# The second half's attention: its scores in pairs of PSUM banks, with one maximum and one exponential for each tile

## The chip, the cores and the metric

The kernel runs on one core of one Trainium2 chip. Its time is the device time of one execution in microseconds (us). The engines are TensorE (PE, with its weight loads as PEld), VectorE (DVE), ScalarE (ACT), GpSimd (POOL) and SyncE (SP), which issues most of the DMAs. Each engine works through a queue of its own in order, and semaphores tie the queues together. TensorE writes into PSUM, which has eight banks of 128 partitions x 512 floats.

## The reference, cut to what matters

One inference step of a decoder layer: 1024 prompt rows of width 1024, and beside them one new row for each of 8 samples, which attend over 8192 past positions in a paged cache. Both groups go through a combined projection, forgetting attention (8 heads of 64) and spatial gating, a merge, cross-attention to 256 memory rows, and a gated MLP of 2816 columns. The change is in the attention of the prompt:

```python
def fox_attend(q, k, v, cq, ck, qpos, kpos):
    s = jnp.einsum('bqhd,bkhd->bhqk', q, k).astype(jnp.float32) * (ATT_HEAD_DIM ** -0.5)
    s = s + (cq.astype(jnp.float32).transpose(0, 2, 1)[:, :, :, None]
             - ck.astype(jnp.float32).transpose(0, 2, 1)[:, :, None, :])
    s = jnp.where(kpos[None, :] <= qpos[:, None], s, -jnp.inf)
    p = jax.nn.softmax(s, axis=-1).astype(v.dtype)
    return jnp.einsum('bhqk,bkhd->bqhd', p, v)
```

cq and ck are running sums of the logarithm of the forget gate. Inputs and outputs are float32.

## The kernel before

**Stages.** The prompt is worked on in two halves of 512 rows. `prompt` (L1701) goes through the projections (p1), the attention of the first half (att0) and of the second (att1), and then for each half the merge with cross-attention (mid0, mid1) and the MLP (ffn0, ffn1). The 8 samples are a background: the main loop lets one step of theirs in whenever the prompt's work has passed a pace that is set for each stage (`PACE`). A step of the samples gathers pages of the cache by GpSimd (L1306 for keys, L1365 for values), multiplies keys and query on VectorE (L1312), sums these products there (L1316), or multiplies values with weights on TensorE (L1371). In att1 the key products and sums are cut into pieces of 1024 elements (`KS` = 2).

**The order of the instructions.** The program is built in a tile framework: the code gives out tiles of named pools, the framework puts a wait wherever a buffer is used again, and a planner that knows costs of its own for the instructions fixes the order of each engine's queue when the kernel is built. The code's order is its start; instructions of different stages and of the background can change places.

**PSUM before.** One pool holds all eight banks: four single banks under the tag `ba` (`BA()`, L115), two under `bb`, one under `ms`, one under `dv`. `BK()` (L123) hands out `ba` and `bb` in turn to the large matmuls of the other stages. A buffer of a tag is given out again once all reads of its last tile are done.

**The attention of a half** (`attention(hf)`, L657; hf = 1 is the second half, rows 512 to 1023). Heads are taken in pairs, hp = 0 to 3, and rows in two blocks (blk) of two query blocks of 128 rows each (ii), for each of the two heads of a pair (j). That makes eight score tiles for each head pair: 640, 768, 640 and 768 keys wide, and then 896, 1024, 896 and 1024; 32 tiles in the half. In the first half of the prompt tiles are 128 to 512 keys wide and fit one bank.

- `setup` (L674) prepares a head pair while the one before it runs: four transposes of q (L677) into a `ba` bank, copies to SBUF on ScalarE (L683, L684), and a subtraction on VectorE (L697) that gives the low parts; then twice, for the two halves of the keys, four transposes (L702) into a `ba` bank, copies on ScalarE (L706), casts on GpSimd (L708) and subtractions on VectorE (L713). Two matmuls with high and low parts then give float32 precision.
- `scores` (L716) makes a tile. Its width is cut into two halves of n = 320, 384, 448 or 512 columns, each in a `ba` bank of its own: matmuls L728 and L730, the causal mask by a matmul L732 on the second half, and a maximum of each half on VectorE (L733). L736 joins the two maxima (they are negated, so by a minimum). Then ScalarE takes the exponential of each half (L738), which adds up its row as it goes; the sums come out with an accumulator read, and lie in `ls`. The result goes to a slot shared with streamed weights (`wr`, four slots).
- `turn` (L749) transposes the exponentials (L756) into `bb` and `ms` banks and copies them out, on ScalarE (L763) or for one in four on VectorE (L761).
- `values` (L765) multiplies with v (L772), copies the result (L781), adds up the halves' sums (L783) and takes the reciprocal (L784); `back` (L787) transposes (L793) and scales (L795).

`turn`, `values` and `back` stand in a list that runs two tiles behind the scores (`LA`), so that between a tile's scores and its transposes the next two tiles' scores are issued:

```python
queue.append(partial(turn, p_, pt[j], nkt - 1 + ii, ii))
...
drain(LA[hf])
yield 1.8
```

Beside att1 runs the end of the first half (`close`, L863, by `beside`, L879), and after it follow the merge (L860) and its output projection (L973 to L975).

Of the kernel before, what the change touches and what calls it, by code (L numbers as in the profile page):

```python
# [7 lines left out]
F32 = mybir.dt.float32  # L8
# [3 lines left out]
AF = mybir.ActivationFunctionType  # L12
ALU = mybir.AluOpType
AX = mybir.AxisListType
PSUM = bass.MemoryType.PSUM
# [3 lines left out]
P = 128  # L19
# [59 lines left out]
def build(nc, tc, ctx, a, phases=None):  # L79
# [8 lines left out]
    psum = ctx.enter_context(tc.tile_pool(name="psum", bufs=1, space=PSUM))  # L88
    dram = ctx.enter_context(tc.tile_pool(name="dram", bufs=1, space=DRAM))

    cnt = [0]

    def nm(s):
        cnt[0] += 1
        return f"{s}_{cnt[0]}"
# [16 lines left out]
    def sm(shape, tag, bufs=2, dt=F32):  # L112
        return small.tile(shape, dt, tag=tag, bufs=bufs, name=nm(tag))

    def BA():  # L115
        return psum.tile([P, 512], F32, tag="ba", bufs=4, name=nm("ba"))

    def BB():
        return psum.tile([P, 512], F32, tag="bb", bufs=2 + MB, name=nm("bb"))
# [537 lines left out]
    def attention(hf, late=None, at=3):  # L657
# [58 lines left out]
        def scores(qkv, ls, blk, j, ii):  # L716

            qab, ka, kb, _ = qkv
            i = blk * 2 + ii
            e = (hf * 4 + i + 1) * P  # L720
            nch = 1 if e <= 512 else 2
            n = e // nch
            p_ = (WRAW(e) if PW else U([P, e])) if hf else T2(e)
            mx = sm([P, 2], "mx", 4)
            tiles = []
            for ch in range(nch):
                s = BA()[:, :n]
                mmul(s, qab[j][:, 0, i * P : (i + 1) * P], ka[j][:, ch * n : ch * n + n], start=True, stop=False)  # L728
                diag = ch == nch - 1
                mmul(s, qab[j][0:68, 1, i * P : (i + 1) * P], kb[j][0:68, ch * n : ch * n + n], start=False, stop=not diag)  # L730
                if diag:
                    mmul(s[:, n - P :], ident_b, cmask_b, start=False, stop=True)  # L732
                nc.vector.tensor_reduce(mx[:, ch : ch + 1], s, axis=AX.X, op=ALU.max, negate=True)  # L733
                tiles.append(s)
            if nch == 2:
                nc.vector.tensor_tensor(mx[:, 0:1], mx[:, 0:1], mx[:, 1:2], op=ALU.min)  # L736
            for ch in range(nch):
                nc.scalar.activation(  # L738
                    p_[:, ch * n : ch * n + n], tiles[ch], AF.Exp, bias=mx[:, 0:1], accum_out=ls[:, ii, j, ch : ch + 1]
                )  # L740
            return p_

# [22 lines left out]
        def values(qkv, ls, pt, hp, blk):  # L765
            vn = qkv[3]
            nkt = hf * 4 + blk * 2 + 2
            po = B3()
            for kt in range(nkt):
                for j in range(2):  # L770
                    q0 = P if kt == nkt - 1 else 0
                    mmul(  # L772
                        po[64 * j : 64 * j + 64, q0:256],
                        vn[:, kt, 64 * j : 64 * j + 64],
                        pt[j][kt // 4][:, kt % 4, q0:256],
                        start=(kt == 0),
                        stop=(kt == nkt - 1),
                        tile_position=(0, 64 * j),
                    )
            ot = T2(256)  # L780
            nc.scalar.activation(ot, po[:, :256], AF.Copy)  # L781
            rl = sm([P, 4], "rl", 3)
            nc.vector.tensor_reduce(rl, ls.rearrange("p i j c -> p (i j) c"), axis=AX.X, op=ALU.add)  # L783
            nc.vector.reciprocal(rl, rl)  # L784
            return ot, rl, hp, blk

        def back(ot, rl, hp, blk):  # L787
# [25 lines left out]
        for hp in range(4):  # L813
            for _ in nxt or ():
                pass
            qkv, nxt = got.pop(), None
            if hp == at and late:
                late()
            for blk in range(2):
                ls = sm([P, 2, 2, 2], "ls", 3)  # L820
                if hf == 0:
                    nc.vector.memset(ls, 0.0)
                pt = []
                nkt = hf * 4 + blk * 2 + 2
                for j in range(2):
                    for ii in range(2):
                        p_ = scores(qkv, ls, blk, j, ii)
                        if ii == 0:
                            pt.append(
                                [  # L830
                                    (U([P, 4, 256]) if nkt - g > 2 else T2(512).rearrange("p (a b) -> p a b", b=256))
                                    for g in range(0, nkt, 4)
                                ]
                            )
                        queue.append(partial(turn, p_, pt[j], nkt - 1 + ii, ii))
                        if j == 1 and ii == 1:

                            def fin(*args):
                                r = values(*args)
                                queue.insert(min(BKQ, len(queue)), partial(back, *r))  # L840

                            queue.append(partial(fin, qkv, ls, pt, hp, blk))
                        drain(LA[hf])
                        yield 1.8
                        if hp < 3 and (blk, j, ii) == LD[hf]:
                            raw = load(hp + 1)
                        if hp < 3 and (blk, j, ii) == ST[hf]:
                            nxt = setup(hp + 1, *raw)
                        if nxt:
                            next(nxt, None)  # L850
                            yield 1
# [11 lines left out]
    def close(hf, att):  # L863

        ssa = sm([P, 4], "ssa", 1)
        for i in range(4):
            ssq_into(ssa[:, i : i + 1], att[i // 2][:, i % 2, :])
        yield
        r = rstd_of(ssa, AW, 4, "ra")
        yield  # L870
        for b2 in range(2):
            for i in range(2):
                t = att[b2][:, i, :]
                nc.vector.tensor_scalar(t, t, r[:, b2 * 2 + i : b2 * 2 + i + 1], None, op0=ALU.mult)
            t0 = hf * 4 + b2 * 2
            nc.sync.dma_start(an_d[t0 * P : (t0 + 2) * P, :].rearrange("(c p) d -> p c d", p=P), att[b2])
        yield

    def beside(main, steps, at):  # L879

        n = 0
        while True:
            try:
                t = next(main)
            except StopIteration as e:
                return e.value
            yield t
            if n in at:
                next(steps)
            n += 1  # L890
# [810 lines left out]
    def prompt():  # L1701
# [26 lines left out]
        ending = close(0, att)  # L1728
        next(ending)
        phase[0] = "att1"  # L1730
        if G0R:
            att = yield from mix(gating(0), att1, 1 / G0R)
        else:
            att = yield from beside(att1, ending, (0, 2))
        ending = close(1, att)
        next(ending)
        ends = []
# [133 lines left out]
```

## Time and profile before

| | |
|---|---|
| median of 3 runs | 1911.37 us (1909.26 to 1916.39) |
| the profiled execution | 1913.18 us, span 1911.4 us |
| mean granted TensorE clock | 0.978 of full speed |
| PE busy | 1816.1 us, 95% of the span |
| PEld busy | 1296.3 us, 68% |
| DVE busy | 1404.6 us, 73% |
| ACT busy | 761.7 us, 40% |
| POOL busy | 480.6 us, 25% |
| moved by DMA | 517.07 MB, 271 GB/s in the mean |

Busy time leaves out register, branch, semaphore and DMA-issuing instructions. In the rows of the profile, `L728 ... ba<-u,u 128*128 128x448 f32` is line 728 with output and input by the names in the code (`ba` is a bank of that tag, `u` a work tile, `wr` a slot for weights and exponentials, `mx` the maxima, `ls` the sums), then the shape of what is written or read. What stands in brackets at the end of a row of the timeline is the time for which the engine was idle just before, and what ended it. In a group, "10.8, 689 | 6.5" is busy time in us, the mean of one instruction in ns, and the engine's idle time ahead of the group. A group's releaser is inferred from semaphores.

### The profile page before, as it was taken

The page shows a single profiled execution, that of the slowest core. Times are in us where ns is not written, and L with a number is a line of the kernel's source. Part 1 is how long each engine was busy: PE and PEld are TensorE (multiplying, and loading weights), DVE is VectorE, ACT ScalarE, POOL GpSimd, SP SyncE. Part 2 cuts the span into 40 slices and gives each one's busy share as a digit, 9 for nine tenths or more (in the row PEclk, how much of TensorE's full clock was granted, in tenths as well). Part 3 has the DMA queues.
Part 4 walks back from the last instruction along what each step waited for, and adds up shares of the span by engine and source line. Part 5 has one row for each costly group of instructions (what it writes and reads, how often), then busy time and mean ns, then how long its engine had stood idle before and what let it go on. Part 6 is the DMA issues. An engine that isn't in the chain of part 4 may idle for free.

```text
span 1911.4 us, 24216 instructions
## 1 busy us (share of the span) xinstructions
PE 1816.1 (95%) x9255; PEld 1296.3 (68%) x9255; DVE 1404.6 (73%) x1662; ACT 761.7 (40%) x1435; POOL 480.6 (25%) x429
## 2 busy tenths in 40 slices
PE   8999999778898999999999999998999999899998
PEld 5987666555676667777777776775665667667765
DVE  4888678777777887989989998887864548754344
ACT  5332356566633435333333244324353333232232
POOL 1232342222121332213432322354222012101110
PEclk9999999989998999999999999998999999899999
DMA  8777988743395876759878879888859557676872
GB/s 322 286 245 278 323 319 302 265 162 119 128 399 210 324 268 256 297 206 359 313 264 313 301 304 344 340 338 302 307 206 362 191 200 265 215 242 247 320 280 101
DMA packets 156373, 517.07 MB, mean 271 GB/s; under 512 B 20169, under 2 KB 41929, under 8 KB 123489
## 3 DMA queue, kind: packets, MB, share of 16 engines
q0 software_dynamic: 56400, 339.04, 47.7%
q1 hardware_dynamic: 92944, 163.89, 24.7%
q10 hardware_dynamic: 6912, 12.59, 1.7%
q8 instruction: 73, 1.20, 0.2%
q14 instruction: 44, 0.35, 0.1%
HBM read 493.63 MB, written 21.84 MB: 270 GB/s over the span
## 4 chain that ended last, share of the span: by engine, by line
PE 66%; DVE 8%; ACT 3%; DMA 3%; issue 2%; POOL 0%; SPq 0%; DVEq 0%; POOLq 0%; ACTq 0%
PE ba L247 9%; PE ba L246 9%; PE ba L248 9%; PE bb L246 6%; PE bb L247 5%; PE bb L248 5%; PE dv L1371 5%; DMA kv<-cache_k,kidx 2%; DVE kv L1312 1%; DVE s L1316 1%; PE dv L1614 1%; PE ba L973 1%; PE ba L975 1%; PE ba L974 1%; PE bb L772 1%
## 5 line engine op out<-in xcount | busy, mean ns | idle before, releaser
L209 ACT ACTIVATE wh<-wr 128x1024 fp32r<-128x1024 f32 (+2 forms) x220 | 228.8, 1044 | 488.8 <-PE ba L247 147.8
L210 DVE TENSOR_TENSOR wl<-wr,wh 128x1024 fp32r<-128x1024 f32 (+2 forms) x220 | 262.5, 1200 | 166.7 <-PE ba L248 71.3
L1306 POOL DMA_INDIRECT kv<-cache_k,kidx x128 | 179.8, 1405 | 545.6 <-DVE s L1316 249.3
L1312 DVE TENSOR_TENSOR kv<-kv,d 128x2048 f32<-128x2048 f32 (+1 forms) x139 | 292.3, 2113 | 28.2 <-DMA kv<-cache_k,kidx 26.9
L1316 DVE TENSOR_REDUCE s<-kv 128x32 f32<-128x2048 f32 (+1 forms) x139 | 292.0, 2106 | 0.6
L1365 POOL DMA_INDIRECT kv<-cache_v,kidx x128 | 181.3, 1416 | 424.2 <-PE dv L1371 169.6
L246 PE MATMUL ba<-wh,u 128*128 128x512 f32 (+1 forms) x596 | 226.9, 382 | 0.0
L247 PE MATMUL ba<-wl,u 128*128 128x512 f32 (+1 forms) x596 | 226.2, 380 | 0.0
L248 PE MATMUL ba<-wh,u 128*128 128x512 f32 (+1 forms) x596 | 223.4, 380 | 1.0 <-DVE u L210 1.0
L246 PE MATMUL ba<-u,wh 128*128 128x512 f32 (+2 forms) x520 | 203.0, 391 | 1.3 <-DVE u L213 1.2
L247 PE MATMUL ba<-u,wh 128*128 128x512 f32 (+2 forms) x520 | 203.8, 392 | 0.0
L248 PE MATMUL ba<-u,wl 128*128 128x512 f32 (+2 forms) x520 | 202.7, 390 | 0.0
L1371 PE MATMUL dv<-kv,s 128*32 128x512 f32 x1024 | 138.0, 618 | 6.8 <-DMA kv<-cache_v,kidx 6.8
L246 PE MATMUL bb<-u,wh 128*128 128x512 f32 (+2 forms) x344 | 138.2, 402 | 1.8 <-DVE u L213 1.8
L247 PE MATMUL bb<-u,wh 128*128 128x512 f32 (+2 forms) x344 | 136.5, 397 | 2.5 <-DVE u L213 2.5
L248 PE MATMUL bb<-u,wl 128*128 128x512 f32 (+2 forms) x344 | 135.9, 396 | 0.0
L246 PEld LDWEIGHTS ba<-wh,u 128*128 128x128 f32 x596 | 112.7, 189 | 31.4 <-issue 8.0
L248 PEld LDWEIGHTS ba<-wh,u 128*128 128x128 f32 x596 | 112.1, 189 | 29.0 <-issue 6.3
L247 PEld LDWEIGHTS ba<-wl,u 128*128 128x128 f32 x596 | 112.4, 189 | 23.8 <-issue 2.9
L247 PEld LDWEIGHTS ba<-u,wh 128*128 128x128 f32 x520 | 98.7, 190 | 33.3 <-issue 13.0
L246 PEld LDWEIGHTS ba<-u,wh 128*128 128x128 f32 x520 | 98.5, 190 | 31.7 <-issue 7.1
L248 PEld LDWEIGHTS ba<-u,wl 128*128 128x128 f32 x520 | 98.5, 189 | 28.5 <-issue 9.3
(418 smaller groups left out, 3105.5 us busy)
## 6 DMA issues: line engine op xcount, KB each, us to landing
wr<-w_up SPq DMA_DIRECT2D x88, 512.0 KB
kv<-w_up POOLq DMA_DIRECT2D x22, 1024.0 KB
wr<-w_down SPq DMA_DIRECT2D x40, 512.0 KB
kv<-w_down POOLq DMA_DIRECT2D x11, 1024.0 KB
wr<-w_in SPq DMA_DIRECT2D x16, 512.0 KB
wr<-w_o SPq DMA_DIRECT2D x16, 512.0 KB
wr<-w_cq SPq DMA_DIRECT2D x16, 512.0 KB
wr<-w_co SPq DMA_DIRECT2D x16, 512.0 KB
```

What stands on the lines that cost most here:

```text
L209: nc.scalar.activation(h, src, AF.Copy)
L210: nc.vector.tensor_tensor(l, src, h.bitcast(F32), op=ALU.subtract)
L246: mmul(out, sh, mh, start=(i == 0), stop=False)
L247: mmul(out, sh, ml, start=False, stop=False)
L248: mmul(out, sl, mh, start=False, stop=(i == n - 1))
L772: mmul(po[64 * j : 64 * j + 64, q0:256], vn[:, kt, 64 * j : 64 * j + 64], pt[j][kt // 4][:, kt % 4, q0:256], start=(kt == 0), stop=(kt == ...
L973: mmul(pss[i], mh[k][:, tb], wh, start=(k == korder[0]), stop=False)
L1306: nc.gpsimd.indirect_dma_start(kv, None, a["cache_k"], off(kidx[:, b, ch : ch + 1]))
L1312: nc.vector.tensor_tensor(kvv[:, i : i + m, :], kvv[:, i : i + m, :], qb.unsqueeze(1).broadcast_to((P, m, 512)), op=ALU.mult)
L1316: nc.vector.tensor_reduce(s[:, ch * 4 + i : ch * 4 + i + m, :].rearrange("p k h -> p (k h)"), kvv[:, i : i + m, :].rearrange("p k (h d) -> ...
L1365: nc.gpsimd.indirect_dma_start(kv, None, a["cache_v"], off(kidx[:, b, ch : ch + 1]))
L1371: mmul(dv[32 * j : 32 * j + 32, :], s[:, ch * 4 : ch * 4 + 4, :].rearrange("p k h -> p (k h)"), kvv[:, j, :], start=(ch == 0), stop=(ch == ...
```

## The change

The four `ba` banks move into a pool of their own, which is opened and closed by `ba_pool`. For all stages but att1 it holds four single banks, as before. Ahead of att1 it is closed and opened again with two tiles of two banks each, and after att1 it goes back to four. With pairs, `BA()` gives the first half of a pair and, if nothing else came between, the second half the next time; `BA2()` gives a whole pair and drops a half left over. The pair is reused as one tile, when all reads of it are done.

In `scores` a tile of the second half takes a pair, each half of its columns in one bank of it. One maximum on VectorE reads both banks, and one exponential on ScalarE reads both and adds up the whole row. The minimum that joined two maxima is gone, and with it the sum over the halves in `values` and the zeroing of `ls` in the first half; the reciprocal reads `ls` itself. The matmuls are the same. The transposes of `setup` take their bank from `BA()` as before, which in att1 is a half of a pair.

```diff
--- before.py
+++ after.py
@@ -88,6 +88,20 @@
     psum = ctx.enter_context(tc.tile_pool(name="psum", bufs=1, space=PSUM))
     dram = ctx.enter_context(tc.tile_pool(name="dram", bufs=1, space=DRAM))
 
+
+    banks, half_ = [], []
+
+    def ba_pool(pairs):
+        half_.clear()
+        if banks:
+            banks.pop()[0].__exit__(None, None, None)
+        if pairs is not None:
+            p = tc.tile_pool(name="ba2" if pairs else "ba1", bufs=1, space=PSUM, reuse_waits="tile")
+            banks.append((p, p.__enter__(), pairs))
+
+    ba_pool(False)
+    ctx.callback(ba_pool, None)
+
     cnt = [0]
 
     def nm(s):
@@ -113,7 +127,16 @@
         return small.tile(shape, dt, tag=tag, bufs=bufs, name=nm(tag))
 
     def BA():
-        return psum.tile([P, 512], F32, tag="ba", bufs=4, name=nm("ba"))
+        if not banks[0][2]:
+            return banks[0][1].tile([P, 512], F32, tag="ba", bufs=4, name=nm("ba"))
+        if half_:
+            return half_.pop()[:, 512:]
+        half_.append(BA2())
+        return half_[0][:, :512]
+
+    def BA2():
+        half_.clear()
+        return banks[0][1].tile([P, 1024], F32, tag="ba", bufs=2, name=nm("ba"))
 
     def BB():
         return psum.tile([P, 512], F32, tag="bb", bufs=2 + MB, name=nm("bb"))
@@ -721,22 +744,22 @@
             nch = 1 if e <= 512 else 2
             n = e // nch
             p_ = (WRAW(e) if PW else U([P, e])) if hf else T2(e)
-            mx = sm([P, 2], "mx", 4)
-            tiles = []
+            mx = sm([P, 1], "mx", 4)
+            both = BA2().rearrange("p (c n) -> p c n", c=2)[:, :, :n] if nch == 2 else BA()[:, :n].unsqueeze(1)
             for ch in range(nch):
-                s = BA()[:, :n]
+                s = both[:, ch, :]
                 mmul(s, qab[j][:, 0, i * P : (i + 1) * P], ka[j][:, ch * n : ch * n + n], start=True, stop=False)
                 diag = ch == nch - 1
                 mmul(s, qab[j][0:68, 1, i * P : (i + 1) * P], kb[j][0:68, ch * n : ch * n + n], start=False, stop=not diag)
                 if diag:
                     mmul(s[:, n - P :], ident_b, cmask_b, start=False, stop=True)
-                nc.vector.tensor_reduce(mx[:, ch : ch + 1], s, axis=AX.X, op=ALU.max, negate=True)
-                tiles.append(s)
-            if nch == 2:
-                nc.vector.tensor_tensor(mx[:, 0:1], mx[:, 0:1], mx[:, 1:2], op=ALU.min)
-            for ch in range(nch):
+            if nch == 1:
+                nc.vector.tensor_reduce(mx, s, axis=AX.X, op=ALU.max, negate=True)
+                nc.scalar.activation(p_[:, :e], s, AF.Exp, bias=mx, accum_out=ls[:, ii, j : j + 1])
+            else:
+                nc.vector.tensor_reduce(mx, both, axis=AX.XY, op=ALU.max, negate=True)
                 nc.scalar.activation(
-                    p_[:, ch * n : ch * n + n], tiles[ch], AF.Exp, bias=mx[:, 0:1], accum_out=ls[:, ii, j, ch : ch + 1]
+                    p_[:, :e].rearrange("p (c n) -> p c n", c=2), both, AF.Exp, bias=mx, accum_out=ls[:, ii, j : j + 1]
                 )
             return p_
 
@@ -780,8 +803,7 @@
             ot = T2(256)
             nc.scalar.activation(ot, po[:, :256], AF.Copy)
             rl = sm([P, 4], "rl", 3)
-            nc.vector.tensor_reduce(rl, ls.rearrange("p i j c -> p (i j) c"), axis=AX.X, op=ALU.add)
-            nc.vector.reciprocal(rl, rl)
+            nc.vector.reciprocal(rl, ls.rearrange("p i j -> p (i j)"))
             return ot, rl, hp, blk
 
         def back(ot, rl, hp, blk):
@@ -817,9 +839,7 @@
             if hp == at and late:
                 late()
             for blk in range(2):
-                ls = sm([P, 2, 2, 2], "ls", 3)
-                if hf == 0:
-                    nc.vector.memset(ls, 0.0)
+                ls = sm([P, 2, 2], "ls", 3)
                 pt = []
                 nkt = hf * 4 + blk * 2 + 2
                 for j in range(2):
@@ -1728,10 +1748,12 @@
         ending = close(0, att)
         next(ending)
         phase[0] = "att1"
+        ba_pool(True)
         if G0R:
             att = yield from mix(gating(0), att1, 1 / G0R)
         else:
             att = yield from beside(att1, ending, (0, 2))
+        ba_pool(False)
         ending = close(1, att)
         next(ending)
         ends = []
```

## The prediction

> **What bounds the kernel now.** I read the page first, then busy time by stretches, then TensorE's waits inside the stretch that the diff touches, then the timeline around the longest of them. The stretch is 390 to 527 us: the profile's first pair of 320-wide score matmuls starts just before it and the last tile's products end with it. In the stretches the columns are start:end, length, busy time of PE, PEld, DVE, ACT and POOL (with instructions), granted TensorE clock, DMA share and GB/s.
>
> ```profile
> span 1911.4 us, 24216 instructions
> PE 1816.1 (95%) x9255; PEld 1296.3 (68%) x9255; DVE 1404.6 (73%) x1662; ACT 761.7 (40%) x1435; POOL 480.6 (25%) x429
> 390.00:527.00 137.00, 111.45 (x751) 77.88 (x750) 99.13 (x201) 88.49 (x235) 29.11 (x37) 0.93 0.43 145
> 620.00:760.00 140.00, 134.70 (x650) 95.26 (x648) 112.67 (x119) 65.37 (x137) 41.91 (x34) 0.99 0.78 291
> ```
>
> TensorE is busy for 95% of the span, and 134.70 of 140.00 us in a stretch after the change: what the second half's attention saves or loses, the rest passes on to the end. In that stage TensorE is idle for 137.00 - 111.45 = 25.55 us, and at a clock of 0.93 a further 111.45 x 0.07 = 7.8 us are lost. These 33 us are all that a better order could win. DMA moves 145 GB/s, so transfers are not the matter. VectorE and ScalarE aren't full, but TensorE waits for them:
>
> ```profile
> PE ba L728 <- DVE mx L736: 6.8, 1, 6.8
> PE ba L728 <- ACT wr L738: 5.6, 6, 1.6
> 416.12 1.29 DVE L733 TENSOR_REDUCE mx<-ba 128x1 f32<-128x512 f32 x2
> 417.32 1.21 DVE L1316 TENSOR_REDUCE s<-kv 128x16 f32<-128x1024 f32 x1
> ...
> 419.98 1.20 DVE L1316 TENSOR_REDUCE s<-kv 128x16 f32<-128x1024 f32 x1
> ...
> 421.82 0.14 DVE L736 TENSOR_TENSOR mx<-mx 128x1 f32<-128x1 f32 x1
> 422.00 0.69 ACT L738 ACTIVATE wr<-ba,mx 128x512 f32<-128x512 f32 x1 [6.02 <-DVE mx L736]
> 422.05 0.71 PE L728 MATMUL ba<-u,u 128*128 128x448 f32 x1 [6.78 <-DVE mx L736]
> ```
>
> The first two rows are total, times and longest. The timeline shows the largest: both maxima of a 1024-wide tile are done by 417.4, but the small minimum that joins them (L736) stands on VectorE behind two halves of the decoder's key products, and everything waits to 422.
>
> **What the change costs and saves, part by part.** In the built program the order of every engine is the one before up to the end of the first half's attention, and again from some 60 us behind the second's (TensorE's first 1788 and last 5170 of 8073 instructions are equal). DMA issues are equal in number; within the stage one V gather moves ahead of two casts (L708) on POOL, and single loads change place with a neighbour on SP. At 145 GB/s I cost that at nothing; were a gather late by one cast, it is 0.65 us.
>
> Fewer instructions. Here and below the form 128x512 is a half of a 1024-wide tile:
>
> ```profile
> L733 DVE TENSOR_REDUCE mx<-ba 128x1 f32<-128x512 f32 x16 | 10.8, 689 | 6.5 <-PE ba L730 3.5 <-PE ba L732 2.7
> L733 DVE TENSOR_REDUCE mx<-ba 128x1 f32<-128x128 f32 x8 | 2.3, 284 | 0.1
> L736 DVE TENSOR_TENSOR mx<-mx 128x1 f32<-128x1 f32 x32 | 4.7, 152 | 0.4
> L783 DVE TENSOR_REDUCE rl<-ls 128x4 f32<-128x8 f32 x9 | 1.4, 157 | 3.9 <-ACT wr L738 3.9
> L738 ACT ACTIVATE wr<-ba,mx 128x512 f32<-128x512 f32 x16 | 10.9, 692 | 10.9 <-DVE mx L736 10.9
> L738 ACT ACTIVATE wr<-ba,mx 128x320 f32<-128x320 f32 x16 | 8.3, 534 | 0.0
> L738 ACT ACTIVATION_READ_ACCUMULATOR wr<-ba,mx 128x1 f32 x64 | 13.3, 208 | 0.0
> L1082 DVE TENSOR_REDUCE cmx<-ba 128x2 f32<-128x512 f32 x12 | 8.1, 684 | 5.5 <-PE ba L1080 3.4 <-issue 2.1
> ```
>
> A maximum costs (689 - 284) / 384 = 1.05 ns per element and 149 ns besides; an exponential (692 - 534) / 192 = 0.82 and 271. So one maximum over a pair of 512 is an estimated 149 + 1.05 x 1024 = 1.23 us and one exponential 271 + 0.82 x 1024 = 1.11. Per tile VectorE saves 149 + 152 = 0.30 us, ScalarE 271 + 208 = 0.48. Over 32 tiles that is 9.6 and 15.3 us; eight L783 add 1.3 (the memsets of ls and L783 in the first half save VectorE little, where TensorE waits for others). None of it is on the path by itself. No row reads two banks at once. Bounds: as dear as two single instructions (1.38 and 1.38 us, so +0.42 us per tile on the chain), or as the fit; L1082, with a grouped read, costs no more than the plain one (684 against 689), so I take the fit.
>
> Later banks. From the tile's last matmul, the first half's bank came free after 0.69 + 0.15 + 0.69 = 1.53 us, now with the second after 1.23 + 1.11 = 2.34. So the first is 0.8 us later, the second about as before. There are two pairs. In the built program each group of transposes that sets up the next head pair (L677 once, L702 twice, three times over) takes one of the two pairs for half its width. TensorE works in order, so behind a waiting score matmul stand the transposes, products and decoder matmuls of other tiles, and VectorE and ScalarE soon wait for those. The places, before:
>
> ```profile
> 401.25 0.44 PE L728 MATMUL ba<-u,u 128*128 128x384 f32 x1 [1.35 <-ACT wr L738]
> 405.11 0.47 PE L728 MATMUL ba<-u,u 128*128 128x448 f32 x1 [0.55 <-ACT wr L738]
> 406.67 1.92 PE L1371 MATMUL dv<-kv,s 128*32 128x512 f32 x16
> 443.82 3.42 PE L772 MATMUL ms<-u,u 128*64 128x256 f32 x16 [2.79 <-ACT t L763]
> 449.72 0.60 PE L702 MATMUL ba<-cp,u 128*128 128x128 f32 x4
> 450.16 0.38 PE L793 MATMUL ms<-cp,t 128*128 128x128 f32 x2
> 450.46 1.20 ACT L706 ACTIVATE u<-ba 64x512 fp32r<-64x512 f32 x2
> 451.69 0.69 ACT L738 ACTIVATE wr<-ba,mx 128x512 f32<-128x512 f32 x1
> 451.72 1.38 DVE L713 TENSOR_TENSOR u<-ba,u 64x512 fp32r<-64x512 f32 x2
> 452.52 0.47 PE L728 MATMUL ba<-u,u 128*128 128x448 f32 x1 [1.56 <-ACT wr L738]
> 474.75 0.65 PE L772 MATMUL bb<-u,u 128*64 128x256 f32 x2 [0.52 <-DVE t L761]
> 476.26 1.72 PE L772 MATMUL bb<-u,u 128*64 128x256 f32 x13 [0.86 <-ACT u L763]
> 483.44 0.47 PE L728 MATMUL ba<-u,u 128*128 128x448 f32 x1 [1.56 <-ACT wr L738]
> 487.17 2.35 DVE L1312 TENSOR_TENSOR kv<-kv,d 128x1024 f32<-128x1024 f32 x2
> 490.83 2.33 DVE L1316 TENSOR_REDUCE s<-kv 128x16 f32<-128x1024 f32 x2
> 494.10 0.65 PE L756 MATMUL bb<-cp,wr 128*128 128x128 f32 x4 [3.96 <-ACT wr L738]
> ```
>
> (a) The second 896-wide tile of head pairs 0, 1 and 2 waited 6.78, 1.56 and 1.56 us. It now lies on the pair of the 1024-wide tile right ahead of it, with only four transposes (449.72 to 450.16, 0.44 us) between. Behind these come two L706 (1.20) on ScalarE, then the exponential (1.11) and a hand-over of 0.14 (451.69 + 0.69 to 452.52): 0.44 + 0.10 + 1.20 + 1.11 + 0.14 = 3.0 from the tile's last matmul, so TensorE is idle for 3.0 - 0.44 = 2.55, three times. The minimum behind the key products is gone, but this comes in its place: 7.65 - 9.90 = -2.25 us.
>
> (b) The value products L772 wait for ScalarE's copies (L763), which stand behind the set-up's four copies: 2.79 us at 443.82, 0.52 + 0.86 at 475, and nothing in head pair 0, where eight decoder matmuls (1.92 at 406.67) filled the time. In the new order these eight stand behind the L772, because the transposes ahead of them need the pair. I take the mean of the two shown, 2.1, three times: 6.3 - 4.2 = +2.1.
>
> (c) The last tile of head pair 2 had its minimum behind two L1312 and two L1316 (487.17 to 493.2); its maximum now stands there in one piece: 2.35 + 2.33 + 1.23 + 1.11 + 0.14 = 7.2 against 494.10 - 487.17 = 6.9: +0.3.
>
> (d) The third and fourth tile (401.25, 405.11) waited 1.35 + 0.55; the first bank comes 0.8 later: +0.8. The first tile needs the bank of the first half's last tile, under seven transposes: nothing; without these, 0.7.
>
> (e) The second L702 group lies on the first one's pair and waits for its L713 (1.38 for two), which it didn't before: between 0 and 1.4 three times; 2.0, since VectorE's queue is long there.
>
> (f) The clock. After a long wait TensorE runs slow for a while:
>
> ```profile
> 400.00:405.00 5.00, 3.30 (x22) 2.54 (x22) 3.17 (x11) 5.00 (x18) 3.97 (x6) 1.00 0.58 204
> 420.00:425.00 5.00, 2.95 (x10) 2.28 (x11) 3.41 (x7) 2.30 (x7) 0.96 (x1) 0.50 0.88 249
> 425.00:430.00 5.00, 4.34 (x30) 3.44 (x29) 2.88 (x9) 3.49 (x10) 0.00 (x0) 0.86 0.64 237
> 450.00:455.00 5.00, 3.44 (x20) 2.52 (x19) 4.29 (x11) 4.34 (x12) 1.22 (x2) 0.87 0.36 110
> ```
>
> The wait of 1.35 us at 401 left it at 1.00; that of 1.56 at 452 was followed by 0.87, that of 6.78 by 0.50 and 0.86. Five waits of 1.56 or more cost the 7.8 us, 1.56 each. Now they are (a) three, (b) three, (c) one: two more, +3.1, less about one share for the 6.78 that becomes 2.55: +1.5. [...]
>
> (g) Shorter queues: each copy that (b) waits for stands behind one exponential, now 0.48 shorter, three times 1.4; the small waits of the stage (25.55 - 9.90 - 4.2 - 3.96 - 1.90 = 5.6 us in about ten) lose an estimated 0.15 each: -2.9 together.
>
> Sum: -2.25 + 2.1 + 0.3 + 0.8 + 2.0 + 1.5 - 2.9 = +1.6 us.
>
> The profiled execution took 1913.18 us, 1.8 more than its span; so 1914.8 for it, and from the median of the runs (1911.37, 0.1% below it) **1913.0**.
>
> **The rivals.**
>
> Faster: the pairs do not bind, and what waited for VectorE and ScalarE gains. For it: 25 us less work on two engines that end nearly all of TensorE's waits. Against it: the order gives (a) new waits where the old went. Priced: 6.78 becomes 2.55 (-4.2), 3.96 becomes 2.5 as the key products slip behind (-1.5), three slow-clock shares go (-4.7): -10.4, 1901.0.
>
> Slower: two pairs are too few. Each of the nine set-up groups holds one, so score tiles go one at a time. Three of the nine are in (a); at the six others TensorE waits a whole 2.34 + 0.14 less some seven transposes (0.11 each, 0.8), 1.7 each, 10.2, and two more slow-clock shares (3.1): +13.3 on the forecast's base, 1924.7. It decides once TensorE has under 2.5 us of other work between two tiles on one pair. Against it: the order puts six to ten transposes and the value products there. [...]
>
> Two-bank reads at the dear end: +0.42 on the chain at about ten waits, +4.2: 1917.2.
>
> It changes nothing at the end, because a later wait takes up the difference: 1911.4. TensorE's 134.70 of 140.00 speaks against it.
>
> **How the numbers follow.** Forecast 0.39, faster rival 0.22, slower rival 0.32, dear reads 0.04, nothing 0.03: the rivals together get more than half, since the terms (b), (e) and (g) are each about as large as the sum. The range takes in both rivals' prices: 1900 to 1926. I leave out 0.2, gains or losses beyond them. [...] About 0.5% (9.6 us) is what a measurement of this kernel can tell from no change. Faster by more: the faster rival, 0.22; slower: the slower one, 0.32; within it the rest, 0.46.
>
> **What would show it.** Right: in the changed profile 32 maxima near 1.23, 1.09, 0.96 and 0.82 us and 32 exponentials near 1.11 to 0.80; VectorE's work in the stage 10 to 11 us less, ScalarE's 15 less; no wait of 6.8 us; three waits near 2.5 on the second 896-wide tile, ended by the exponential; L772 waiting in head pair 0; a stage of 137 us within 4, at a clock of 0.91 to 0.94. Wrong: idle time below 18 or above 36 us in the stage, or a difference that arises outside it.

## The result, and the profile after

The changed kernel takes 1903.99 us (median of 14 runs, 1895.07 to 1908.88) against 1910.84 us for the kernel before beside it (14 runs, 1906.80 to 1916.39): a ratio of 0.995, 95% interval 0.9939 to 0.9961 (the two medians alone give 0.9964). By the medians it is some 7 us faster, at the edge of the 0.5% that the prediction took as the least that can be told. The forecast was 1913.0, slower by 1.6 us; the time lies in the range, on the other side. The profiled execution took 1899.86 us, 4 us less than the median, so what follows looks at stretches and not at its span alone.

The first line of the page, and the stretches, which are cut here for each kernel by its own landmarks: from the first 320-wide score matmul to the end of the last products (the attention), and from the first matmul of the first output projection to that of the second (behind the attention). First the kernel before, with columns as in the prediction:

```profile
389.20:525.90 136.70, 111.15 (x749) 77.46 (x747) 99.28 (x201) 88.38 (x235) 29.11 (x37) 0.93 0.42 142
526.70:690.00 163.30, 153.07 (x733) 108.47 (x731) 127.24 (x137) 68.98 (x141) 39.55 (x31) 0.97 0.81 302
```

The changed kernel:

```profile
span 1898.1 us, 24082 instructions
```

and its stretches:

```profile
388.90:520.50 131.60, 111.92 (x732) 79.41 (x731) 88.74 (x126) 79.55 (x164) 31.93 (x37) 0.90 0.43 146
521.20:679.60 158.40, 152.51 (x732) 108.91 (x731) 127.19 (x137) 69.12 (x140) 45.96 (x31) 0.98 0.84 311
```

The attention lasts 131.6 us and not 136.7: TensorE's idle time in it fell from 25.55 to 19.68 us, while the mean granted clock fell from 0.93 to 0.90. The stretch behind lasts 158.4 and not 163.3, though VectorE does the same work there (127.19 against 127.24 us in 137 instructions). So in this profile nearly as much was gained in a stretch where the code wasn't touched as in the attention.

The new instructions, by line and shape, are as large as the prediction's fit made them (1.23 and 1.11 us for 1024 elements, 0.82 for the maximum of 640):

```profile
L760 DVE TENSOR_REDUCE mx<-ba 128x1 f32<-128x1024 f32 x8 | 9.8, 1224 | 3.8 <-PE ba L755 3.7
L760 DVE TENSOR_REDUCE mx<-ba 128x1 f32<-128x640 f32 x8 | 6.5, 814 | 6.0 <-PE ba L755 6.0
L761 ACT ACTIVATE wr<-ba,mx 128x1024 f32<-128x1024 f32 x8 | 8.9, 1114 | 2.7 <-DVE mx L760 2.5
```

TensorE's timeline of the changed kernel, the rows with a wait (rows between them are left out); L751 is a score matmul, L779 a transpose of exponentials, L795 a value product, L725 the second key transpose of the set-up:

```profile
399.37 0.47 PE L751 MATMUL ba<-u,u 128*128 128x448 f32 x1 [0.78 <-ACT wr L761]
402.32 0.65 PE L795 MATMUL bb<-u,u 128*64 128x256 f32 x2 [1.13 <-ACT t L786]
403.56 3.17 PE L795 MATMUL bb<-u,u 128*64 128x256 f32 x13 [0.59 <-ACT u L786]
...
415.93 0.47 PE L751 MATMUL ba<-u,u 128*128 128x448 f32 x1 [3.03 <-ACT wr L761]
418.73 0.77 PE L751 MATMUL ba<-u,u 128*128 128x512 f32 x1 [0.25 <-DVE u L736]
...
439.95 1.95 PE L795 MATMUL ms<-u,u 128*64 128x256 f32 x16 [1.85 <-ACT t L786]
446.08 0.63 PE L725 MATMUL ba<-cp,u 128*128 128x128 f32 x4 [0.96 <-DVE u L736]
449.24 0.74 PE L751 MATMUL ba<-u,u 128*128 128x448 f32 x1 [2.53 <-ACT wr L761]
...
473.39 1.73 PE L795 MATMUL bb<-u,u 128*64 128x256 f32 x13 [0.92 <-ACT u L786]
479.40 0.63 PE L725 MATMUL ba<-cp,u 128*128 128x128 f32 x4 [0.83 <-DVE u L736]
482.56 0.74 PE L751 MATMUL ba<-u,u 128*128 128x448 f32 x1 [2.53 <-ACT wr L761]
...
491.75 1.10 PE L779 MATMUL bb<-cp,wr 128*128 128x128 f32 x8 [1.09 <-ACT wr L761]
```

The wait of 6.78 us is gone, and three of 3.03, 2.53 and 2.53 stand on the second 896-wide tile, as forecast. What is not as forecast is the last row: 1.09 us where the kernel before had 3.96. VectorE's timeline of the changed kernel at that place:

```profile
486.97 2.35 DVE L1332 TENSOR_TENSOR kv<-kv,d 128x1024 f32<-128x1024 f32 x2
489.24 1.22 DVE L760 TENSOR_REDUCE mx<-ba 128x1 f32<-128x1024 f32 x1
490.38 2.34 DVE L1336 TENSOR_REDUCE s<-kv 128x16 f32<-128x1024 f32 x2
```

The two key products still come first, but the maximum now stands ahead of the two key sums, and the exponential can start before these. In the kernel before the second of the tile's two maxima stood in the same place, but the minimum that joins them came behind the sums:

```profile
489.44 1.48 DVE L733 TENSOR_REDUCE mx<-ba 128x1 f32<-128x512 f32 x3
493.09 0.22 DVE L736 TENSOR_TENSOR mx<-mx 128x1 f32<-128x1 f32 x2
```

At the first place, too, the key sums were only a part of what stood between. Of the 4.4 us from the maxima (done at 417.41) to the minimum (421.82), two key sums took 2.4; the rest was a maximum of the next tile, two scalings of earlier results and two subtractions of the set-up.

### The profile page after: what moved, and what is told of

Its sections match the earlier page's. It is cut to its first block, busy times and chain, and to the rows that moved or that the text cites. A ratio compares the mean times of both kernels' runs of the same rounds, so it can differ in the third digit from the quotient of the medians.

```text
span 1898.1 us, 24082 instructions
## 1 busy us (share of the span) xinstructions
PE 1817.0 (96%) x9255; PEld 1299.4 (68%) x9255; DVE 1394.5 (73%) x1574; ACT 755.7 (40%) x1371; POOL 490.6 (26%) x429
## 4 chain that ended last, share of the span: by engine, by line
PE 82%; DVE 8%; ACT 4%; DMA 3%; issue 2%; POOL 0%; SPq 0%; DVEq 0%; POOLq 0%; ACTq 0%
PE ba L270 12%; PE ba L269 12%; PE ba L271 12%; PE bb L269 7%; PE bb L270 7%; PE bb L271 7%; PE dv L1391 6%; DVE kv L1332 2%; DMA kv<-cache_k,kidx 1%; PE dv L1634 1%; PE bb L795 1%; PE ba L993 1%; PE ba L994 1%; PE ba L995 1%; DVE wl L233 1%
## 5 line engine op out<-in xcount | busy, mean ns | idle before, releaser
L1326 POOL DMA_INDIRECT kv<-cache_k,kidx x128 | 185.7, 1451 | 528.6 <-DVE s L1336 241.7
```

Of the source, the lines that this page charges most:

```text
L1326: nc.gpsimd.indirect_dma_start(kv, None, a["cache_k"], off(kidx[:, b, ch : ch + 1]))
```

## The experiments

Two theories were set against each other. **Order**: the gain is the join. A minimum of 0.15 us behind the maxima gave the planner a place in VectorE's queue to put 2.4 us of key sums, and more, in between; without it the exponential follows the maximum. And behind the attention the queue came out in another order, by which TensorE waits less. **Work**: VectorE and ScalarE have 10 and 9 us less to do in the attention, and every wait for them gets shorter, there and behind. Times are medians; the kernel before ran beside each set, and its medians (1910.21 to 1911.85) are within 1.7 us of one another. The length of a stretch is that of one execution, and the last run below shows that it can differ by some 5 us between executions of one kernel. An edit can also move other instructions in the planner's queues, so hardly a run changes one thing alone.

### One maximum, two exponentials

```diff
             nc.vector.tensor_reduce(mx, both, axis=AX.XY, op=ALU.max, negate=True)
-            nc.scalar.activation(p_[:, :e]..., both, AF.Exp, bias=mx, accum_out=ls[:, ii, j : j + 1])
+            for ch in range(2):
+                nc.scalar.activation(p_[:, ch * n : ch * n + n], both[:, ch, :], AF.Exp, bias=mx, accum_out=ls[:, ii, j, ch : ch + 1])
```

> The changed kernel with its pairs and its one maximum, but two exponentials and the sum over the halves as before. VectorE's work is that of the changed kernel (only the eight sums come back), ScalarE gets its 15 us back. In the built program VectorE's queue in the attention is close to the changed kernel's (no minimum to stand behind the key products), but behind the attention it has the key products where the kernel before has them. Theory order (the gain is 5.5 us in the attention, because nothing that joins two halves stands behind the key products any more, and 4.8 us in the 60 us behind it, because the key products come at other places among VectorE's weight splits): the attention ends some 4 to 5 us earlier than before, the stretch behind it gains nothing, about 1906 to 1907. Rival work (fewer instructions on VectorE and ScalarE shorten every wait for them, in the attention and behind it): VectorE's saving is kept, so the stretch behind the attention keeps its gain, and the attention loses ScalarE's part: also some 1906, but with TensorE idle for about 4 us between 527 and 620 us and not for 8.

1905.28 us, a ratio to the kernel before of 0.9973 (0.996 to 0.9986). The stretches:

```profile
391.70:519.10 127.40, 108.04 (x732) 73.47 (x731) 89.73 (x134) 86.85 (x227) 31.14 (x37) 0.96 0.45 153
519.80:683.60 163.80, 153.66 (x733) 110.11 (x731) 127.30 (x137) 69.05 (x141) 40.42 (x31) 0.96 0.80 300
```

In the attention it is as good as the changed kernel with ScalarE's time given back, and behind it nothing is gained (163.80, before 163.30). Between 527 and 620 us TensorE is idle for 8.2 us. That is the sign that the order theory had named (8 us, against 4 by the other).

### Two maxima and the minimum, one exponential

```diff
-            nc.vector.tensor_reduce(mx, both, axis=AX.XY, op=ALU.max, negate=True)
+            for ch in range(2):
+                nc.vector.tensor_reduce(m2[:, ch : ch + 1], both[:, ch, :], axis=AX.X, op=ALU.max, negate=True)
+            nc.vector.tensor_tensor(mx, m2[:, 0:1], m2[:, 1:2], op=ALU.min)
```

> The changed kernel with its pairs and its one exponential, but two maxima and the minimum that joins them. VectorE gets 9.6 us back, ScalarE keeps its saving. In the built program the minimum stands behind two key sums and the two subtractions of the set-up again, in head pair 0 and at the last tile of head pair 2. Theory order: the two long waits are back (some 6 and 4 us of TensorE), and the exponential over both banks makes them longer by up to 0.4 us: 1910 to 1914. Rival work: ScalarE's 15 us are the larger half of what was saved, so at least half of the gain stays, 1907 or less.

1920.23 us, ratio 1.0048 (1.0029 to 1.0066). The attention lasts 143.9 us, 7.2 more than before the change. TensorE's waits from 385 to 530 us, the longest groups (total, times, longest):

```profile
PE ba L751 <- ACT wr L764: 9.6, 6, 2.6
PE bb L782 <- ACT wr L764: 8.1, 4, 4.4
PE ba L751 <- DVE mx L763: 5.9, 1, 5.9
```

The minimum (L763 here) is waited for again, 5.9 us, and the wait of the last tile of head pair 2 is 4.4; the waits for pairs are there beside them (9.6). The sign is as the order theory had it, the size is larger than its 1910 to 1914: the pairs and the join add up. Saving ScalarE half of its exponentials gained nothing.

### Pairs alone

Both edits above together, so that in the second half only the banks, and the queues that follow from them, differ from the kernel before.

> Pairs of banks alone: two maxima, the minimum and two exponentials on the halves of a pair, as before the change. What is left of the change is that a tile's first bank comes free with its second, and that the set-up's transposes take a pair. Theory order: as long as the kernel before or longer, since the minimum stands behind the key products and both banks now wait for it: 1911 to 1916. Rival work: the same sign, as nothing is saved: 1911 to 1914. A time below 1908 would say that the pairs themselves, by the order that they give, are what made it faster.

1918.81 us, ratio 1.0043 (1.0029 to 1.0057), the attention 145.2 us. VectorE's timeline ahead of the second 896-wide tile of head pair 0 shows the join at work (L1344 are key sums, L736 subtractions of the set-up, L763 the minimum):

```profile
422.13 1.29 DVE L762 TENSOR_REDUCE m<-ba 128x1 f32<-128x512 f32 x2
...
423.73 2.33 DVE L1344 TENSOR_REDUCE s<-kv 128x16 f32<-128x1024 f32 x2
425.98 1.38 DVE L736 TENSOR_TENSOR u<-ba,u 64x512 fp32r<-64x512 f32 x2
427.28 0.14 DVE L763 TENSOR_TENSOR mx<-m 128x1 f32<-128x1 f32 x1
```

and TensorE's the wait that it ends:

```profile
427.51 0.71 PE L751 MATMUL ba<-u,u 128*128 128x448 f32 x1 [6.19 <-DVE mx L763]
```

Pairs, with the queues that go with them, cost some 7 us, more than either theory had forecast (up to 1916). Behind the attention this kernel takes 157.8 us, with all of VectorE's work back: its queue happens to have the changed kernel's order there.

### VectorE's time given back

```diff
             nc.vector.tensor_reduce(mx, both, axis=AX.XY, op=ALU.max, negate=True)
+            nc.vector.tensor_copy(gv[:, 0:1], mx)
+            nc.vector.tensor_tensor(gv[:, 1:2], mx, gv[:, 0:1], op=ALU.min)
```

> The changed kernel with two small VectorE instructions more for each tile, a copy and a minimum on 128x1 behind the maximum, which nobody waits for: VectorE's 0.30 us for each tile are given back. In the built program the queues behind the attention are those of the changed kernel up to the second half's MLP. Theory order: within 2 us of the changed kernel, 1903 to 1906. Rival work: most of the gain behind the attention and a part of that in it goes, 1908 to 1911.

1900.77 us, ratio 0.9948 (0.993 to 0.9967): nothing of the gain is lost. The stretches:

```profile
389.90:516.70 126.80, 106.16 (x732) 75.40 (x731) 95.74 (x190) 79.26 (x164) 31.91 (x37) 0.95 0.44 152
517.40:675.10 157.70, 150.55 (x731) 106.08 (x730) 126.84 (x137) 68.92 (x140) 48.51 (x31) 1.00 0.85 314
```

VectorE works 95.74 us in an attention of 126.8, which gives back 7 of the 10.5 us that it had saved, and neither stretch is longer for it; the time is below both forecasts. The saved time of VectorE was worth nothing by itself, and the run with two exponentials says the same of ScalarE's: the work theory falls.

### No join, single banks

```diff
-            if nch == 2:
-                nc.vector.tensor_tensor(mx[:, 0:1], mx[:, 0:1], mx[:, 1:2], op=ALU.min)
...
-                    p_[...], tiles[ch], AF.Exp, bias=mx[:, 0:1], accum_out=...
+                    p_[...], tiles[ch], AF.Exp, bias=mx[:, ch : ch + 1], accum_out=...
```

> The kernel before, with four single banks, two maxima and two exponentials, but without the minimum that joins the maxima: each half takes the exponential with its own maximum, so the rows are scaled wrongly. 32 instructions of 0.15 us leave VectorE. Theory order (it is the join behind the key products that costs, not the number of instructions or the banks): the waits of 6.8 and 4.0 us shrink to under 2 each and single banks make no new ones, so the attention gains at least the 7 us that the changed kernel gains there with pairs; the place of the key products behind it is near that of the kernel before, so nothing is gained there: 1902 to 1906. Rival (the pairs, or the shorter queue of ScalarE, are what helps): at most 2 us, 1909 to 1912.

1895.69 us, ratio 0.9913 (0.9895 to 0.993), more than forecast: 16 us for 32 instructions of 0.15 us. The attention lasts 125.5 us, the stretch behind 162.5, near the kernel before. Its longest waits from 385 to 530 us are

```profile
PE ms L770 <- ACT t L761: 2.8, 1, 2.8
PE ba L728 <- ACT wr L736: 2.6, 5, 0.8
```

(lines as in the kernel before, less the two that went: L736 is the exponential). No score matmul waits longer than 0.8 us. So four single banks without the join do as well in the attention as pairs (125.5 against 131.6 and 126.8 us in two profiles). The 16 us aren't the price of the key sums in between alone: without the join the first half's exponential needn't wait for the second half's maximum either, so it can start, and its bank come free, sooner. No run separates the two.

### The changed kernel with its maximum at a higher priority

```diff
-            nc.vector.tensor_reduce(mx, both, axis=AX.XY, op=ALU.max, negate=True)
+            with tc.high_priority():
+                nc.vector.tensor_reduce(mx, both, axis=AX.XY, op=ALU.max, negate=True)
```

> The changed kernel with its maximum under a higher priority. In the built program the attention's queues hardly move (two neighbours on VectorE in head pair 3), but VectorE's order behind the attention falls back to that of the kernel before: the fourth weight split stands behind a key product again. All instructions are those of the changed kernel. Theory order: the attention as in the changed kernel, TensorE idle for some 8 us between 527 and 620 us as before the change: 4 to 5 us longer than the changed kernel, 1905 to 1909. Rival work: the same work, so the same time as the changed kernel within 2 us and TensorE idle for some 4 us there.

1909.49 us, ratio 0.9989 (0.9976 to 1.0002). The stretches:

```profile
391.80:517.80 126.00, 105.12 (x731) 74.42 (x730) 88.71 (x126) 79.48 (x163) 31.08 (x37) 0.96 0.45 152
518.60:682.20 163.60, 152.07 (x733) 108.24 (x730) 127.34 (x137) 69.26 (x141) 39.34 (x31) 0.97 0.80 302
```

The same instructions, the same attention, and 5 us more behind it: there the queues have nearly the order of the kernel before. The difference is one of order alone, but not of VectorE's alone, as TensorE's and ScalarE's instructions in this stretch stand in another order than in the changed kernel too.

In VectorE's queue the sign of it is short. After the decoder's L1298 the queue has three weight splits, a key product, and the fourth split in six of the eleven kernels (before, one maximum, one exponential, this one, and the kernel before with another set-up below; the one without a join has two, the product, and two): these take 162.0 to 164.2 us behind the attention, and TensorE is idle there for 10.1 to 11.5 us. The others (the changed kernel, pairs alone, VectorE's time given back, and the two set-ups below) have four splits in a row, and the product later: 157.7 to 158.9 us, with TensorE idle for 5.9 to 8.2. In VectorE's timeline of the kernel before (L210 is the split, L1312 the product):

```profile
578.31 2.29 DVE L1312 TENSOR_TENSOR kv<-kv,d 128x2048 f32<-128x2048 f32 x1
580.51 1.22 DVE L210 TENSOR_TENSOR wl<-wr,wh 128x1024 fp32r<-128x1024 f32 x1
```

and in TensorE's the waits between 575 and 610 us:

```profile
582.38 1.95 PE L1007 MATMUL ba<-cp,u 128*128 128x128 f32 x9 [2.06 <-DVE u L932]
586.15 0.69 PE L246 MATMUL bb<-u,wh 128*128 128x384 f32 x1 [1.81 <-DVE u L213]
594.72 1.13 PE L582 MATMUL ba<-u,u 128*128 128x128 f32 x8 [1.70 <-issue]
...
605.94 0.33 PE L247 MATMUL bb<-u,wh 128*128 128x128 f32 x1 [2.51 <-DVE u L213]
```

The changed kernel, in the same place:

```profile
577.66 1.48 PE L1027 MATMUL ba<-cp,u 128*128 128x128 f32 x6 [2.18 <-DVE u L236]
588.18 0.48 PE L1043 MATMUL ba<-cp,u 128*128 128x128 f32 x1 [1.86 <-DVE u L236]
```

The product of 2.29 us holds up the split and, behind that, the subtraction L932, and TensorE waits 2.06 us. But the changed kernel has waits of about that size as well, since there the product stands ahead of other work that TensorE needs. What it is without are the last two waits of the kernel before, 1.70 and 2.51 us, the 4 us by which its idle time is smaller. So the place of the fourth split tells the two orders apart; that it is what costs the time isn't shown.

### The set-up's transposes in other banks

```diff
-            tr = (MS, BB, BA)[SB]()
+            tr = (MS if hf else BA)()      # and, in the second kernel, (BB if hf else BA)()
```

> The changed kernel with the set-up's transposes of the second half in the single ms bank, so that pairs hold scores alone. In the built program VectorE's order behind the attention is the changed kernel's. The three waits of 3.0, 2.5 and 2.5 us of the second 896-wide tile and the three of 0.3 to 1.0 of the second key transposes should go, 9.9 us together; in their place the transposes of the exponentials and the value products have to share ms with the set-up, which holds it for the copies and two subtractions, some 3 us each of nine times. If the pairs bind (the rival of the forecast that was priced at 1924.7, in its reverse): 4 to 8 us shorter than the changed kernel, 1896 to 1900. If ms binds instead: the same or up to 6 us longer, 1904 to 1910.

> As the last, with the set-up's transposes in the two bb banks. There are two of these, so the exponentials' transposes find one of them free more often than ms: if the pairs bind, 4 to 8 us shorter than the changed kernel, 1896 to 1900, and not longer than with ms; if the exponentials' transposes wait for the set-up's bank, 1904 to 1910.

In ms: 1910.61 us, ratio 0.9991 (0.9976 to 1.0007), the attention 132.3 us; score matmuls wait for the exponential in three places only, 1.0 us in all, but in ms a value product waits 2.8 us for a subtraction of the set-up and a transpose 2.0 us. In bb: 1894.17 us, ratio 0.9913 (0.9897 to 0.9929), the fastest kernel here that does the whole computation, and below its forecast. Its attention:

```profile
392.10:508.80 116.70, 103.22 (x736) 72.43 (x735) 89.18 (x126) 78.77 (x165) 32.52 (x37) 0.99 0.50 165
```

and its longest group of waits from 385 to 530 us:

```profile
PE ba L751 <- ACT wr L761: 4.6, 6, 1.5
```

Now no wait is longer than 1.6 us, the clock stays at 0.99, and the attention takes 116.7 us, 20 less than before the change. The three waits of 3.03, 2.53 and 2.53 us for a pair, while the set-up held the other, are gone: there two pairs did bind in the changed kernel.

> The kernel before, with single banks, two maxima, the minimum and two exponentials, and with the set-up's transposes of the second half in the two bb banks. With pairs this step was worth some 10 us. If it is worth that because the set-up took pairs from the scores, it is worth little here, where it only took one of four single banks and the minimum still stands behind key sums in places: 1907 to 1911. If bb is the better place for any kernel, 1900 to 1903.

The same edit in the kernel before gives 1902.08 us, ratio 0.9953 (0.9936 to 0.9969), with an attention of 124.8 us. The expectation that it is worth little without pairs was wrong, and the other, that bb is the better place for any kernel, came true: the step is worth some 8 us here and some 10 with pairs, and step and change add up within their intervals (0.995, 0.9953, together 0.9913). So the 10 us can't be put down to the pairs that came free. Which part is the bank and which the new order of the queues, no run here separates.

This kernel also bears on the join, which it keeps. On VectorE a minimum stands 3.8 us behind its two maxima:

```profile
438.64 1.27 DVE L733 TENSOR_REDUCE mx<-ba 128x1 f32<-128x512 f32 x2
439.83 2.33 DVE L1316 TENSOR_REDUCE s<-kv 128x16 f32<-128x1024 f32 x2
...
443.69 0.16 DVE L736 TENSOR_TENSOR mx<-mx 128x1 f32<-128x1 f32 x1
```

Yet TensorE's next wait is one of 0.44 us at 447.96, and it is for a subtraction. So a late join doesn't cost by itself. It costs where TensorE has no other work left, as in the two places of the kernel before (6.78 and 3.96 us).

### The changed kernel once more

> The changed kernel once more, for a second profile. Its waits in the attention are those of the kernel with two small VectorE instructions more, and yet its attention lasted 3.8 us longer, with the granted clock at 0.90 against 0.95. If that is how the clock's steps happened to fall in that execution, another execution has the same waits within 1 us and another clock between 0.89 and 0.96; if it belongs to the kernel, 0.90 again.

1900.86 us, from a single run. Its waits are those of the first profile (9.0 us in 5 waits for pairs, the longest 3.0; TensorE idle for 20.9 us in all, before 19.7). Its stretches, then one around the value products of head pair 0 and one behind the wait of 3.03 us:

```profile
391.10:517.90 126.80, 105.94 (x731) 75.33 (x730) 88.75 (x125) 79.30 (x163) 31.85 (x37) 0.95 0.44 152
518.60:677.50 158.90, 150.69 (x733) 106.07 (x731) 126.70 (x137) 68.92 (x140) 50.39 (x31) 1.00 0.83 311
405.90:409.30 3.40, 3.40 (x34) 2.03 (x36) 2.24 (x5) 1.50 (x4) 0.00 (x0) 1.00 0.29 108
417.30:420.70 3.40, 3.40 (x14) 2.80 (x13) 3.35 (x5) 1.10 (x2) 0.96 (x1) 0.50 1.13 350
```

and the same two places in the first profile of it:

```profile
403.70:407.10 3.40, 3.40 (x18) 1.94 (x19) 2.29 (x5) 0.80 (x2) 0.00 (x0) 0.50 0.27 100
417.30:427.60 10.30, 9.57 (x37) 7.55 (x35) 5.78 (x8) 5.25 (x10) 0.96 (x1) 0.50 0.73 260
```

The clock differed between the two executions: the attention took 131.6 us at 0.90 in the one and 126.8 at 0.95 in the other, with the same queues and nearly the same waits.

## Why the prediction was wrong

**The direction** came from a sum in which gains and losses of a few us met, and two of its terms had the wrong size, one of them zero.

- Step (c), the last tile of head pair 2, is the step that failed in the attention. The forecast put the whole maximum behind both key products and both key sums: 4.3 us of idle TensorE. In the changed queue it stands between them, and 1.09 us were measured (1.42 in the second execution). The forecast had seen the mechanism at the first place (the minimum behind the key products) and missed that its removal applies here too. The runs with and without the join show that this is the heart of the gain in the attention: with pairs and a join 1918.81 us (attention 145.2), with pairs and one maximum 1905.28 (127.4).
- Behind the attention the forecast had nothing, with the reason that the order of every engine is that of before "again from some 60 us behind". These 60 us were left unpriced, a term put at nothing. The stretch that they are part of holds 4.9 us of the gain (163.3 to 158.4), and the kernel with the maximum at a higher priority shows that it is the order of the queues there. Its "wrong" sign, a difference that arises outside the stage, has come true.
- Step (a) held: 3.03, 2.53 and 2.53 us against three times 2.55. Step (e) held: 0.25 + 0.96 + 0.83 = 2.04 us against 2.0. The fit for one instruction over two banks held (1.224 us against 1.23 for the maximum of 1024 elements, 1.114 against 1.11 for the exponential), and dear reads are out.
- Step (b), less the 1.4 us that step (g) takes off it, came near: the value products waited 1.13 + 0.59, 1.85 and 0.92 us, 4.5 in all against 4.9. Step (d) was too dear: 0.78 us against 2.7; the later release of the first bank was not felt there.
- Step (g) had a wrong price in it: ScalarE saves about 0.25 us for a tile and not 0.48, and 8.8 us in the stage and not 15. The prediction added up the durations of exponentials and accumulator reads, but their records overlap. Before the change the first exponential of a 1024-wide tile starts at 422.00 and lasts 0.69 us, but its read starts at 422.58 and the second exponential at 422.68. So two exponentials and two reads took 1.45 us from start to end, and the one pair of the changed kernel takes 1.21 (490.49 to 491.70). The small waits fell all the same, by 2.4 us and not by 1.5, from 5.6 to 3.2 (19.68 less the 16.5 of (a) to (e)).
- Step (f), the clock, forecast at +1.5 us, cannot be read from one execution: TensorE's busy time in the attention was 111.92 and 105.94 us in two executions of the changed kernel, against 111.15 before.

In sum the attention gained 5.1 and 9.9 us in two executions (forecast: a loss of 1.6) and the stretch behind it 4.9 and 4.4 (forecast: nothing). The rest of the kernel differs by -3 and +2 us in these executions, beside a median that fell by 7. The signs "a stage of 137 us within 4" and "a clock of 0.91 to 0.94" failed (131.6 and 126.8 us, 0.90 and 0.95).

**The rivals.** The faster one, priced at 1901.0, came nearest in time. Its term for the last tile of head pair 2 had the right sign (3.96 becomes 2.5, measured 1.09), but it too left out the stretch behind the attention, and less work wasn't the reason: with most of VectorE's work given back the kernel is as fast. So that its time is so near is in part luck. The one of too few pairs held a true part: the changed kernel waits three times for a pair, 8.1 us in all. It failed as a forecast because it had TensorE wait at the six other set-ups too, and because what was gained at the join was larger. What the pairs cost in the end stays open: the set-up in bb is worth 10 us with them (1894.17 against 1903.99) and 8 without.

## What to carry to other kernels

A small instruction that joins two partial results can cost far more than its duration: when a queue is ordered by a planner, whatever is ready slips between the parts and the join, and where no other work is left the chain waits for it (taking away 32 minima of 0.15 us, and with them the wait of one half for the other, gained 16 us here). Merge the parts, or keep the filler out, and look in the queue for what stands between. Before pricing a change at nothing outside its stage, compare the queues until they are equal again, and price every reordering in that stretch by the same means as in the stage. When buffers are merged into fewer, larger ones, try the small users in other buffers; where they go matters (in bb it gained 10 us, in ms it lost some 6).

## What the runs showed of the hardware

In the attention of the kernel before and of the changed kernel's first profile the granted TensorE clock is at 0.50 in a few stretches and at 1.00 between them. In the kernel before it is at 0.50 once for 6.8 us (from 419.5) and four times for 3.4 us (from 443.4, 453.6, 484.5 and 494.6); in the changed kernel for 3.4, 10.3, 6.8 and 6.8 us (from 403.7, 417.3, 448.1 and 482.2), 27.3 in all, and in its second profile for 3.4, 3.4 and 6.8 us (from 417.3, 448.0 and 478.7), 13.6 in all. So the same waits were followed by different stretches. After waits of 1.13 and 0.59 us TensorE ran at 0.50 for 3.4 us in one execution of the changed kernel and at 1.00 in another (1.12 and 0.59 us); after the wait of 3.03 us it ran at 0.50 for 10.3 us in the one and 3.4 us in the other. The attention lasted 4.8 us longer in the one (131.6 against 126.8) and TensorE was busy 6.0 us longer in it (111.92 against 105.94); such differences may be a part of the changed kernel's spread of 14 us over its runs. The prediction's 1.56 us for each longer wait was a mean over five waits of the kernel before, and these two executions show no fixed price for a wait. In the one profile of the set-up in bb, with no wait over 1.6 us, the clock was 0.99; but in the kernel before a wait of 1.56 us was followed by 0.87 in the stretch from 450 to 455 us.
